# Two value products of the first key block joined into one over two segments, and issued behind both score steps of their slot

## The chip, the cores and the metric

The kernel runs on one core of a Trainium2 chip. The metric is the device time of one execution in microseconds, as the median of several runs. The engines named below are PE (TensorE, with its weight loads listed apart as PEld), DVE (VectorE), ACT (ScalarE), POOL (GpSimd), and SP, whose queue issues most of the DMAs.

## The reference

Two encoder layers over 512 tokens of width 1024, in float32. Each layer has an attention part with two groups of heads that read the same normed input, and a dense part.

```
s  = einsum('bhmqd,bhmkd->bhmqk', q, k) * scale          # differential group: 4 heads, 2 maps each
p  = softmax(where(chunk(k) <= chunk(q), s, min))
out = (p[:, :, 0] - lam * p[:, :, 1]) @ v                # v is 128 wide
z  = einsum('bhqd,bhkd->bhqk', q, k) * scale             # stick-breaking group: 8 heads
w  = where(k < q, sigmoid(z) * exp(sum of log_sigmoid(-z) over the keys between), 0)
out = w @ v                                              # v is 64 wide
```

Both groups are causal (the differential group by chunks of 64 keys), so a block of 128 queries needs only the key blocks up to its own. The outputs of both groups are joined, multiplied by `w_o` and added to x; then follow a norm, a product with 1024x4096 weights, a squared ReLU, and a product back to 1024.

## The kernel before, in words

Products are made of two or three matmuls on fp32r halves: a value is split into a high part (ACT rounds it) and a low part (DVE subtracts), and `three` (L297 to L301) issues high by high, high by low, low by high.

**Dense work and attention share PE.** In each layer the projections (`p..d1q`, `p..s0k`, `p..u` and so on) and the output projection `wo` are a generator of steps of three matmuls or so. The attention is a second generator, `attn` (L732). A loop pays out credit for each dense step and takes attention steps as long as there is credit, so on PE an attention piece is usually followed by 3 to 9 dense matmuls. The Tile layer then sets the final order on each engine by its own estimate of when things are ready; on PE it keeps nearly the written order, on DVE and ACT it moves more.

**Attention by slots.** A layer has 24 units: the 4 differential heads (kind d) with two halves of the queries each, then the 8 stick-breaking heads (kind s) with two halves each. The half 0 is queries 0 to 255, the half 1 queries 256 to 511. Slot i does three things:

- scores of unit i (`s1_df`, `s1_sb`): two or four products into PSUM tiles S, each followed by DVE and ACT work (for d: a maximum on DVE, an exp on ACT, then a combination on DVE; for s: two sigmoids on ACT, a scan on DVE, a product on POOL). Each score step is one step of the generator.
- turning of unit i-2 (`s2`): transposes on PE into the PSUM tiles T, which ACT and DVE split into SBUF tiles of turned weights. xh and xl (896 wide) hold key block 0 of half 0 at columns 0 to 255, key block 1 at 256 to 639, and key block 0 of half 1 at 640 to 895; zh and zl hold key blocks 2 and 3. There is one buffer of each.
- values of unit i-3 (`s3`): products of v with the turned weights into a PSUM tile O (one bank). Half 0 does key block 0 for queries 0 to 255. Half 1, one slot later, does key block 0 for queries 256 to 511 and key block 1 first, then blocks 2 and 3, and evicts O.

So slots with an odd i do the values of a half 0, and slots with an even i, from slot 4, those of a half 1. In such an even slot the generator `attn` interleaves: first score step, values of blocks 0 and 1, second score step, turning, values of blocks 2 and 3.

**PSUM.** The tiles S have three banks in rotation. The transposes of the head norms (rs_d, rb_d) take banks from the same three. A tile takes the bank of the third tile before it, and its first product waits until that tile's last reader is done: the exp or the second sigmoid on ACT for S, the reduction `ms<-rs_d` on DVE for rs_d, and the copy `rb` on ACT for rb_d.

**Weights.** Each dense unit's weights come by DMA (raw), ACT rounds them (whi, L116) and DVE subtracts (wlo, L132). whi and wlo have two buffers, so whi of a unit waits for the last product that reads whi two units before.

Of the kernel before, what the change touches and what calls it, by code (L numbers as in the profile page):

```python
# [9 lines left out]
F32 = mybir.dt.float32  # L10
F32R = mybir.dt.float32r
BF16 = mybir.dt.bfloat16
AF = mybir.ActivationFunctionType
# [4 lines left out]
P = 128  # L18
S = 512
# [12 lines left out]
LAG2, LAG3, KSB = 2, 3, 8  # L32
MTB = 1
# [131 lines left out]
def trunk(ctx, tc, opened, xT, w, w2, w1, gfin, lamv, cos, sin, out):  # L165
    nc = tc.nc
# [23 lines left out]
    x = cp.tile([P, KC, S], F32, tag="x", name="x")  # L190
# [38 lines left out]
    gsub = cp.tile([P, L], F32, tag="gsub", name="gsub")  # L229
# [7 lines left out]
    def split(hi, lo, src):  # L237
        a = nc.scalar.activation(hi, src, AF.Copy)  # L238
        nc.vector.tensor_tensor(out=lo, in0=src, in1=hi.bitcast(F32), op=ALU.subtract)  # L239
        return a  # L240
# [94 lines left out]
    for l in range(L):  # L335
        with ExitStack() as actx:
            am = actx.enter_context(tc.tile_pool(name=f"am{l}", bufs=1))
            ap_ = actx.enter_context(tc.tile_pool(name=f"at{l}", bufs=1))
            a2 = actx.enter_context(tc.tile_pool(name=f"a2{l}", bufs=2))
            a3 = actx.enter_context(tc.tile_pool(name=f"a3{l}", bufs=2))  # L340
# [122 lines left out]
            heads = {}  # L463
# [174 lines left out]
                yield (0.77 if half else 0.33) + (also() if also else 0.0)  # L638

            def s3(u, parts_):  # L640
                half, b, m, kind = u["half"], u["b"], u["m"], u["kind"]
                key = (kind, b, m)
                if half == 0:
                    heads[key] = bank("o", f"O{l}{kind}{b}{m}")
                k = 2 if kind == "s" else 3
                cost = 0.0
                for kb in parts_:
                    t, at_, to, w = {
                        (0, 0): ((xh, xl), 0, 0, 256), (1, 0): ((xh, xl), 640, 256, 256), (1, 1): ((xh, xl), 256, 128, 384),
                        (1, 2): ((zh, zl), 256, 256, 256), (1, 3): ((zh, zl), 0, 256, 256)}[(half, kb)]  # L650
                    o = heads[key][:, to : to + w]
                    wh, wl = (e[:, at_ : at_ + w] for e in t)
                    if kind == "s":
                        v = vs[:, kb, 2 * b + m, :]
                        nc.tensor.matmul(o, v, wh, start=(half == 0), stop=False)
                        nc.tensor.matmul(o, v, wl, start=False, stop=(kb == 3))
                    else:
                        three(o, (vd_hi[:, kb, b * P : (b + 1) * P], vd_lo[:, kb, b * P : (b + 1) * P]), (wh, wl),
                              half == 0, kb == 3)
                    cost += w * k * MMC  # L660
                if half == 1 and parts_[-1] != 3:
                    yield cost
                    return
                if half == 1:
                    o = heads.pop(key)
                    if kind == "s":
                        if m == 0:
                            heads[("mt", b)] = a2.tile([P, S], F32, tag="mt", name=f"mt{l}{b}", bufs=MTB)
                        mt = heads[("mt", b)]
                        oc = tt(f"oc{l}{b}{m}")[0:64, :]  # L670
                        nc.scalar.copy(oc, o[64:128, :])
                        nc.vector.tensor_add(mt[64 * m : 64 * m + 64, :], o[0:64, :], oc)
                        if m == 1:
                            split(ms_hi[:, b, :], ms_lo[:, b, :], mt)
                    else:
                        os_ = a2.tile([P, S], F32, tag="mt", name=f"os{l}{b}", bufs=MTB)
                        sqo = tt(f"sqo{l}{b}")
                        nc.scalar.activation(sqo, o, AF.Square)
                        nc.scalar.activation(os_, o, AF.Copy, scale=gsub[:, l : l + 1])
                        rc = a3.tile([P, 4], F32, tag="rc", name=f"rc{l}{b}")  # L680
                        late.append((b, os_, sqo, rc))
                yield cost

            units = []
# [13 lines left out]
            late = []  # L698
# [29 lines left out]

            def values(u, parts_):
                while not ok(("v" + u["kind"], u["b"])):  # L730
                    yield 0
                yield from s3(u, parts_)  # L732

            def attn():
                n = len(units)
                stage = 0
                for i in range(n + LAG3):
                    stage = stage + 1 if late else 0
                    rest = behind_scores(i, stage)
# [110 lines left out]
        with ExitStack() as fctx:  # L850
# [343 lines left out]
            for g in range(GROUPS):  # L1194
# [184 lines left out]
```

## Time and profile before

| | us |
|---|---|
| median of 3 runs | 1125.02 |
| lowest and highest run | 1124.52, 1125.22 |
| the profiled execution | 1125.43 |
| its span, first to last instruction | 1123.7 |
| PE busy in it | 1115.3 |
| DVE busy | 905.5 |
| ACT busy | 683.8 |
| POOL busy | 155.7 |

The first layer's attention fills 43 to 215 us of the span, that of the second layer 597 to 771 us. Times in rows of the timeline are from the start of the span. A matmul's row shows its start and a modelled duration; what a matmul costs a busy PE is the distance from its start to the next one's. "[0.72 <-PE p0u L438]" behind a row is the idle time of the engine before it and what ended it. Buffer numbers are left out of the names in the profile, while the lists of order below keep them (S0d_1057 is one tile).

### The profile page before, as it was taken

To read this page: it belongs to the slowest core of one execution; us is meant where nothing else is said; L and a number is where in the kernel's file an instruction comes from. 1 tells how busy PE (TensorE), PEld (TensorE's weight loads), DVE (VectorE), ACT (ScalarE), POOL (GpSimd) and SP (SyncE) were. 2 spreads that over 40 slices of the span, in tenths; PEclk is the share of its full clock that TensorE was granted. 3 is DMA by queue.
4 is the path that set the end of the run, shared out by engine and by line. 5 is a ranking of instruction groups with operands and counts; after the bars stand their busy time and mean duration, and the time that the engine had idled before them with its cause. 6 is when DMAs were issued, how large, how long until landed. Compare 5 with 4: busy or idle time off the path is not lost.

```text
span 1123.7 us, 17281 instructions
## 1 busy us (share of the span) xinstructions
PE 1115.3 (99%) x6421; PEld 979.2 (87%) x6421; DVE 905.5 (81%) x1309; ACT 683.8 (61%) x1107; POOL 155.7 (14%) x233
## 2 busy tenths in 40 slices
PE   9999999999999999999999999999999999999997
PEld 7889889888899899899878898988887998998986
DVE  7788789798668779778877887898877787797787
ACT  6446666667558457467344666665765584674665
POOL 1001344101001001001000014430010110010010
PEclk9999999999999999999999999999999999999999
DMA  7466343268687678748325654522477886687462
GB/s 256 129 190 185 113 135 111 75 226 224 175 213 183 175 192 187 190 131 218 101 75 155 191 146 132 165 61 72 150 193 212 213 188 174 186 185 205 115 131 94
DMA packets 61044, 181.26 MB, mean 161 GB/s; under 512 B 7456, under 2 KB 8736, under 8 KB 60960
## 3 DMA queue, kind: packets, MB, share of 16 engines
q1 hardware_dynamic: 50160, 141.84, 39.6%
q0 software_dynamic: 10368, 37.75, 18.9%
q8 instruction: 51, 0.84, 0.3%
q10 hardware_dynamic: 432, 0.56, 0.1%
q14 instruction: 33, 0.27, 0.1%
HBM read 150.77 MB, written 4.19 MB: 138 GB/s over the span
## 4 chain that ended last, share of the span: by engine, by line
PE 92%; DVE 3%; DMA 2%; issue 1%; ACT 1%; POOL 0%; POOLq 0%; DVEq 0%; ACTq 0%
PE X L299 9%; PE X L301 9%; PE X L300 9%; PE V L299 3%; PE V L301 3%; PE V L300 3%; PE wo L299 3%; PE wo L300 3%; PE wo L301 3%; PE Y L301 2%; PE Y L299 2%; PE Y L300 2%; DMA q<-in_w 2%; DVE wlo L132 1%; PE f L299 1%; PE f L300 1%
## 5 line engine op out<-in xcount | busy, mean ns | idle before, releaser
L116 ACT ACTIVATE whi<-q 128x1024 fp32r<-128x1024 f32 x96 | 101.5, 1059 | 110.9 <-PE X L301 38.3
L132 DVE TENSOR_TENSOR wlo<-q,whi 128x1024 fp32r<-128x1024 f32 x96 | 117.0, 1222 | 50.6 <-ACT whi L116 50.5
L132 DVE TENSOR_TENSOR wlo<-raw,whi 128x1024 fp32r<-128x1024 f32 (+1 forms) x82 | 99.1, 1215 | 9.5 <-ACT whi L116 9.0
L116 ACT ACTIVATE whi<-raw 128x1024 fp32r<-128x1024 f32 (+1 forms) x82 | 80.7, 993 | 33.4 <-issue 9.9
L299 PE MATMUL X<-whi,Ah 128*128 128x512 f32 x248 | 97.7, 394 | 0.2 <-DVE y L1107 0.2
L300 PE MATMUL X<-wlo,Ah 128*128 128x512 f32 x248 | 96.7, 390 | 0.0
L301 PE MATMUL X<-whi,Al 128*128 128x512 f32 x248 | 96.7, 390 | 0.0
L132 DVE TENSOR_TENSOR wlo<-waves,whi 128x1024 fp32r<-128x1024 f32 x40 | 48.9, 1222 | 16.5 <-ACT whi L116 16.4
L116 ACT ACTIVATE whi<-waves 128x1024 fp32r<-128x1024 f32 x40 | 42.2, 1055 | 29.1 <-PE X L301 18.2
L299 PEld LDWEIGHTS X<-whi,Ah 128*128 128x128 f32 x248 | 46.6, 188 | 12.1 <-DVE y L1107 2.0
L301 PEld LDWEIGHTS X<-whi,Al 128*128 128x128 f32 x248 | 46.6, 188 | 9.9
L300 PEld LDWEIGHTS X<-wlo,Ah 128*128 128x128 f32 x248 | 46.6, 188 | 8.9
L301 PE MATMUL X<-h_hi,wlo 128*128 128x256 f32 x192 | 54.3, 283 | 0.0
L299 PE MATMUL X<-hxh,whi 128*128 128x256 f32 x192 | 54.3, 283 | 0.0
L300 PE MATMUL X<-hxl,whi 128*128 128x256 f32 x192 | 54.3, 283 | 0.0
L301 PE MATMUL X<-hxh,wlo 128*128 128x256 f32 x192 | 54.3, 283 | 0.0
L300 PE MATMUL X<-h_lo,whi 128*128 128x256 f32 x192 | 54.3, 283 | 0.0
L299 PE MATMUL X<-h_hi,whi 128*128 128x256 f32 x192 | 54.3, 283 | 0.0
L299 PE MATMUL f<-h_hi,whi 128*128 128x512 f32 x128 | 50.3, 393 | 0.0
L301 PE MATMUL f<-h_hi,wlo 128*128 128x512 f32 x128 | 49.9, 390 | 0.0
L300 PE MATMUL f<-h_lo,whi 128*128 128x512 f32 x128 | 49.8, 389 | 0.0
L239 DVE TENSOR_TENSOR Al<-x,Ah 128x512 fp32r<-128x512 f32 (+1 forms) x60 | 46.6, 793 | 3.8 <-ACT Ah L238 3.5
(748 smaller groups left out, 3726.4 us busy)
## 6 DMA issues: line engine op xcount, KB each, us to landing
raw<-in_w SPq DMA_DIRECT2D x78, 512.0 KB, 3.6
q<-in_w SPq DMA_DIRECT2D x48, 512.0 KB, 4.2
q<-in_w POOLq DMA_DIRECT2D x48, 512.0 KB, 7.8
waves<-in_w SPq DMA_DIRECT2D x28, 512.0 KB, 4.4
first_a<-in_w SPq DMA_DIRECT2D x12, 512.0 KB, 4.6
first_b<-in_w SPq DMA_DIRECT2D x12, 512.0 KB, 5.6
first_c<-in_w SPq DMA_DIRECT2D x12, 512.0 KB, 4.2
first_b<-in_w POOLq DMA_DIRECT2D x12, 512.0 KB, 7.0
```

The lines of the kernel that those rows point to most:

```text
L116: return self.nc.scalar.activation(o, src, AF.Copy)
L132: self.last = h, nc.vector.tensor_tensor(out=lo[:, a:b], in0=raw[:, a:b], in1=hi[:, a:b].bitcast(F32), op=ALU.subtract)
L239: nc.vector.tensor_tensor(out=lo, in0=src, in1=hi.bitcast(F32), op=ALU.subtract)
L299: nc.tensor.matmul(pt, ah, bh, start=first, stop=False, skip_group_check=goes_on),
L300: nc.tensor.matmul(pt, ah, bl, start=False, stop=False, skip_group_check=goes_on),
L301: nc.tensor.matmul(pt, al, bh, start=False, stop=last, skip_group_check=goes_on))
```

## The change

Three things are changed, all in the attention part.

1. The four tiles xh, xl, zh and zl become parts of one tile `turned_` (2816 wide). That makes it possible to address the two places of key block 0 (columns 0 to 255 and 640 to 895) as one operand of two segments, `firsts`.
2. The values of half 0 are gone as a step of their own. Half 1 multiplies key block 0 for all 512 queries in one product over the two segments. For a d head three matmuls of 256 columns and three more of 256 become three of 512; for an s head two and two become two.
3. In the even slots that do values (`lead`), the generator issues the first score step, the second score step, then the values of blocks 0 and 1, the turning, and the values of blocks 2 and 3. In odd slots no values are left.

```diff
-            xh, xl = (ap_.tile([P, 896], F32R, tag=f"x{n}", name=f"x{n}{l}") for n in "hl")
-            zh, zl = (ap_.tile([P, 512], F32R, tag=f"z{n}", name=f"z{n}{l}") for n in "hl")
+            turned_ = ap_.tile([P, 2816], F32R, tag="turned", name=f"turned{l}")
+            xh, xl, zh, zl = (turned_[:, a:b] for a, b in ((0, 896), (896, 1792), (1792, 2304), (2304, 2816)))
+            firsts = [turned_[:, a : a + 1280].rearrange("p (a t) -> p a t", a=2)[:, :, 0:256] for a in (0, 896)]
...
             def s3(u, parts_):
-                half, b, m, kind = u["half"], u["b"], u["m"], u["kind"]
+                b, m, kind = u["b"], u["m"], u["kind"]
                 key = (kind, b, m)
-                if half == 0:
+                if parts_[0] == 0:
                     heads[key] = bank("o", f"O{l}{kind}{b}{m}")
                 k = 2 if kind == "s" else 3
                 cost = 0.0
                 for kb in parts_:
-                    t, at_, to, w = {
-                        (0, 0): ((xh, xl), 0, 0, 256), (1, 0): ((xh, xl), 640, 256, 256), (1, 1): ((xh, xl), 256, 128, 384),
-                        (1, 2): ((zh, zl), 256, 256, 256), (1, 3): ((zh, zl), 0, 256, 256)}[(half, kb)]
-                    o = heads[key][:, to : to + w]
-                    wh, wl = (e[:, at_ : at_ + w] for e in t)
+                    if kb == 0:
+                        o, w, (wh, wl) = heads[key], S, firsts
+                    else:
+                        t, at_, to, w = {
+                            1: ((xh, xl), 256, 128, 384), 2: ((zh, zl), 256, 256, 256), 3: ((zh, zl), 0, 256, 256)}[kb]
+                        o = heads[key][:, to : to + w]
+                        wh, wl = (e[:, at_ : at_ + w] for e in t)
...
             def behind_scores(i, stage):
                 n = len(units)
                 u = units[i - LAG3] if 0 <= i - LAG3 < n else None
-                if u and u["half"] == 1:
+                u = u if u and u["half"] else None
+                if u:
                     yield from values(u, (0, 1))
...
                 if u:
-                    yield from values(u, (2, 3) if u["half"] else (0,))
+                    yield from values(u, (2, 3))
...
                         front = (s1_sb if u["kind"] == "s" else s1_df)(u)
+                        lead = i >= LAG3 and units[i - LAG3]["half"]
                         for cost in front:
                             if i == 7 and len(u["w"]) == 2:
                                 table(AF.Sigmoid, ends["exp"])
                             yield cost
+                            if lead:
+                                lead = 0
+                                continue
                             nxt = 0
```

PE in slot 6 of the first layer (the fourth differential head begins; the values are those of the second head). Before, the products of the tile S0d_1082 are followed by dense products p0u and the values O0d_1046; the second score step, S0d_1145, comes only after 22 dense and 6 value products:

```order
L544 MATMUL S0d_1082<-st0d3k,st0d3q 128x128
L436 MATMUL p0u_1106<-whi_992,h_hi 128x256
L437 MATMUL p0u_1106<-wlo_993,h_hi 128x256
L545 MATMUL S0d_1082<-kl0d3k,st0d3q 128x128
L438 MATMUL p0u_1106<-whi_992,h_lo 128x256
L436 MATMUL p0u_1106<-whi_992,h_hi 128x256
L437 MATMUL p0u_1106<-wlo_993,h_hi 128x256
L438 MATMUL p0u_1106<-whi_992,h_lo 128x256
L299 MATMUL O0d_1046<-xh_142,vdh_140 128x256
```

Now, with the numbers of the tiles shifted (S0d_1072 is the first step's tile, S0d_1111 the second's):

```order
L545 MATMUL S0d_1072<-st0d3k,st0d3q 128x128
L438 MATMUL p0u_1096<-wlo_979,h_hi 128x256
L439 MATMUL p0u_1096<-whi_978,h_lo 128x256
L437 MATMUL p0u_1096<-whi_978,h_hi 128x256
L438 MATMUL p0u_1096<-wlo_979,h_hi 128x256
L439 MATMUL p0u_1096<-whi_978,h_lo 128x256
L546 MATMUL S0d_1072<-kl0d3k,st0d3q 128x128
L437 MATMUL p0u_1096<-whi_978,h_hi 128x256
L545 MATMUL S0d_1111<-st0d3k,st0d3q 128x256
```

The second score step now follows one dense product behind the first. The values (three of 512 columns, then three of 384) come 11 dense products later.

ACT at the same place. Before, the exp of S0d_1057, the third tile before S0d_1145, stands ahead of the rounding of a weight unit:

```order
L601 ACTIVATE p0d_1036,sm0d_978<-S0d_1033,sm0d_978 128x384
L601 ACTIVATE p0d_1060,top_867<-S0d_1057,sm0d_1056 128x512
L116 ACTIVATE whi_1108<-raw_892 128x1024
L601 ACTIVATE p0d_1070,sm0d_1056<-S0d_1067,sm0d_1056 128x512
L238 ACTIVATE hl0s0q<-t0s0k 128x512
```

Now (S0d_1044 is that third tile before, whose bank S0d_1111 takes):

```order
L602 ACTIVATE p0d_1033,sm0d_987<-S0d_1030,sm0d_987 128x384
L116 ACTIVATE whi_1098<-raw_869 128x1024
L602 ACTIVATE p0d_1047,top_874<-S0d_1044,sm0d_1043 128x512
L238 ACTIVATE hl0s0q<-t0s0k 128x512
L602 ACTIVATE p0d_1060,sm0d_1043<-S0d_1057,sm0d_1043 128x512
```

The rounding of the weights has moved ahead of the exp whose end frees the bank. The raw weights of that unit replace those of the unit p0s0k, which is two units back.

DVE in slot 11 (the norm of the fourth differential head is begun; the reduction of rs_d_1632 frees a bank of the same three). Before:

```order
L562 TENSOR_SCALAR C0s_1608<-keep0s_1606,edge 128x384
L487 TENSOR_SCALAR t0s2q<-p0s2q,norms 128x512
L132 TENSOR_TENSOR wlo_1647<-raw_1432,whi_1646 128x1024
L239 TENSOR_TENSOR xl_143<-T0s_1617,xh_142 128x512
L239 TENSOR_TENSOR zl_145<-T0s_1618,zh_144 128x384
L273 TENSOR_REDUCE ms<-rs_d_1632 128x4
```

Now:

```order
L488 TENSOR_SCALAR t0s2q<-p0s2q,norms 128x512
L132 TENSOR_TENSOR wlo_1609<-raw_1420,whi_1608 128x1024
L563 TENSOR_SCALAR C0s_1596<-keep0s_1594,edge 128x384
L239 TENSOR_TENSOR hl0s2q<-t0s2q,hl0s2q 128x512
L239 TENSOR_TENSOR turned_142<-T0s_1617,turned_142 128x512
L239 TENSOR_TENSOR turned_142<-T0s_1618,turned_142 128x384
L273 TENSOR_REDUCE ms<-rs_d_1632 128x4
```

One more subtraction of 128x512 (hl0s2q) has moved ahead of the reduction, and on ACT the rounding of that unit's weights stands ahead of the two sigmoids of S0s_1603 where it stood behind them before. The tile that takes the bank of rs_d_1632 is that of slot 12's second score step.

More of the change, by code (lines that the diff above doesn't have):

```diff
@@ L647, in s3 @@
                 for kb in parts_:
-                    t, at_, to, w = {
-                        (0, 0): ((xh, xl), 0, 0, 256), (1, 0): ((xh, xl), 640, 256, 256), (1, 1): ((xh, xl), 256, 128, 384),
-                        (1, 2): ((zh, zl), 256, 256, 256), (1, 3): ((zh, zl), 0, 256, 256)}[(half, kb)]
-                    o = heads[key][:, to : to + w]
-                    wh, wl = (e[:, at_ : at_ + w] for e in t)
+                    if kb == 0:
[5 more added lines that the diff above has]
+                        wh, wl = (e[:, at_ : at_ + w] for e in t)
                     if kind == "s":
                         v = vs[:, kb, 2 * b + m, :]
-                        nc.tensor.matmul(o, v, wh, start=(half == 0), stop=False)
+                        nc.tensor.matmul(o, v, wh, start=kb == 0, stop=False)
                         nc.tensor.matmul(o, v, wl, start=False, stop=(kb == 3))
@@ L658, in s3 @@
                         three(o, (vd_hi[:, kb, b * P : (b + 1) * P], vd_lo[:, kb, b * P : (b + 1) * P]), (wh, wl),
-                              half == 0, kb == 3)
+                              kb == 0, kb == 3)
                     cost += w * k * MMC
-                if half == 1 and parts_[-1] != 3:
+                if parts_[-1] != 3:
                     yield cost
                     return
[L664 to L681, printed above, removed]
@@ new lines, in s3 @@
+                o = heads.pop(key)
+                if kind == "s":
+                    if m == 0:
+                        heads[("mt", b)] = a2.tile([P, S], F32, tag="mt", name=f"mt{l}{b}", bufs=MTB)
+                    mt = heads[("mt", b)]
+                    oc = tt(f"oc{l}{b}{m}")[0:64, :]
+                    nc.scalar.copy(oc, o[64:128, :])
+                    nc.vector.tensor_add(mt[64 * m : 64 * m + 64, :], o[0:64, :], oc)
+                    if m == 1:
+                        split(ms_hi[:, b, :], ms_lo[:, b, :], mt)
+                else:
+                    os_ = a2.tile([P, S], F32, tag="mt", name=f"os{l}{b}", bufs=MTB)
+                    sqo = tt(f"sqo{l}{b}")
+                    nc.scalar.activation(sqo, o, AF.Square)
+                    nc.scalar.activation(os_, o, AF.Copy, scale=gsub[:, l : l + 1])
+                    rc = a3.tile([P, 4], F32, tag="rc", name=f"rc{l}{b}")
+                    late.append((b, os_, sqo, rc))
```

## Prediction

> **What bounds the kernel now.** I read the page first, for the engine without slack.
>
> ```profile
> span 1123.7 us, 17281 instructions
> ...
> PE 1115.3 (99%) x6421; PEld 979.2 (87%) x6421; DVE 905.5 (81%) x1309; ACT 683.8 (61%) x1107; POOL 155.7 (14%) x233
> ...
> PEclk9999999999999999999999999999999999999999
> ...
> PE 92%; DVE 3%; DMA 2%; issue 1%; ACT 1%; POOL 0%; POOLq 0%; DVEq 0%; ACTq 0%
> ```
>
> PE is busy 99% of the span at full clock, and 92% of the chain that ended last is PE. A change pays or costs only by what it takes off PE's own work and by the waits it brings to PE. Busy time of the stretches of the first attention shows what stands closest behind PE.
>
> ```profile
> core 0: us, PE busy (x) PEld busy (x) DVE busy (x) ACT busy (x) POOL busy (x), PEclk, DMA share, GB/s
> 70.00:104.00 34.00, 34.00 (x209) 30.44 (x208) 31.38 (x83) 20.70 (x57) 1.79 (x2) 1.00 0.73 206
> 104.00:146.00 42.00, 42.00 (x257) 37.47 (x256) 32.02 (x56) 28.50 (x59) 13.97 (x20) 1.00 0.35 107
> ```
>
> PE has no gap there, so no value product and no score step waits today. DVE is busy 31.38 of 34 us from 70 to 104 us. There the differential heads' scores need their maximum on DVE and their exp on ACT before a bank is free, and a score step that comes earlier finds a DVE with 8% to spare.
>
> **Step 1, fewer and wider products.** The price of a matmul on a busy PE is the distance of starts. The timeline of PE where a half 0 and then a half 1 of values stood:
>
> ```profile
> 114.88 0.28 PE L299 MATMUL O0d<-xh,vdh 128*128 128x256 f32 x1
> 115.00 0.28 PE L300 MATMUL O0d<-xl,vdh 128*128 128x256 f32 x1
> ...
> 115.23 0.34 PE L299 MATMUL O0d<-xh,vdh 128*128 128x384 f32 x1
> 115.41 0.34 PE L300 MATMUL O0d<-xl,vdh 128*128 128x384 f32 x1
> ...
> 115.76 0.39 PE L299 MATMUL p0s1q<-h_hi,whi 128*128 128x512 f32 x1
> 115.99 0.40 PE L300 MATMUL p0s1q<-h_lo,whi 128*128 128x512 f32 x1
> ```
>
> 256 columns take 0.12 us, 384 take 0.18, 512 take 0.23. Joined are 4 d heads with 3 pairs and 8 s heads with 2 pairs, 28 pairs a layer and 56 in all. A pair goes from 2 x 0.12 = 0.24 to 0.23 us. At 0.24 - 0.227 (the median distance I get behind a 512-wide `three` is 227 ns; the row above, rounded, gives 0.23) a pair saves 13 ns, **56 x 0.013 = 0.73 us**. No row has an operand of two segments. Its bounds are 0.227 us (a plain 512) and 0.24 us (the two it replaces), so the saving lies between 0 and 0.73 us; I take 0.73, since two runs of 256 neighbouring columns resemble the plain 512. All of it lies on the path, because PE has no gap.
>
> The Trainium skill's page "TensorE: Matmul & The Clock Gate", section "Back-to-back issue gap", gives a sustained spacing of about 131 ns for N=512 and 81 ns for N=128 in streams of weight load and matmul. Taken halfway for 256 columns that is an estimate of 65 ns saved a pair, 3.6 us in all. The rows here, 0.23 us for 512, do not agree, and I go by them.
>
> **Step 2, values moved from odd slots into even ones.** The turned weights of half 0 are read one slot later. They are overwritten only after a turning that stands behind these values on PE, so no new wait. O is claimed two score steps later than before, behind the same eviction, so that cover grows. The wider product needs the same tiles that key block 0 of half 1 needed. No DMA is issued by the step. Cost 0.
>
> **Step 3, the second score step ahead of the values.** Each S tile takes the bank of the third before it. Summing row distances in the two orders from a tile's last product to the first product that takes its bank, the room shrinks in slot 6 from 5.8 to 2.7 us and in slot 8 from 4.9 to 2.7; for the bank of rs_d in slots 10 and 12 it falls from 7.3 and 6.2 to 4.0. Four places a layer are tight, and I walk each one.
>
> *Slot 6.* Before, PE, ACT and the claim:
>
> ```profile
> 94.90 0.39 PE L300 MATMUL p0s0k<-h_lo,whi 128*128 128x512 f32 x1
> 95.13 0.39 PE L301 MATMUL p0s0k<-h_hi,wlo 128*128 128x512 f32 x1
> 95.36 0.22 PE L544 MATMUL S0d<-st0d3k,st0d3q 128*128 128x128 f32 x1
> ...
> 99.54 0.28 PE L544 MATMUL S0d<-st0d3k,st0d3q 128*128 128x256 f32 x1
> ```
> ```profile
> 94.72 0.69 ACT L601 ACTIVATE p0d<-S0d,sm0d 128x512 f32<-128x512 f32 x1 [0.41 <-DVE sm0d L607]
> ...
> 95.40 1.05 ACT L116 ACTIVATE whi<-raw 128x1024 fp32r<-128x1024 f32 x1
> 96.35 0.67 ACT L601 ACTIVATE p0d<-S0d,sm0d 128x512 f32<-128x512 f32 x1
> ```
>
> The exp that frees the bank ended at 95.41, and the claim came at 99.54: 4.1 us to spare. Now whi stands ahead of that exp, and whi cannot start before the last product that reads the buffer's old contents (L300 of p0s0k) is through. In slot 4 such a whi started 0.48 us after such a product:
>
> ```profile
> 77.82 0.39 PE L300 MATMUL p0d3k<-h_lo,whi 128*128 128x512 f32 x1
> ```
> ```profile
> 78.30 1.06 ACT L116 ACTIVATE whi<-raw 128x1024 fp32r<-128x1024 f32 x1 [0.37 <-ACT p0d L601]
> 79.26 0.67 ACT L601 ACTIVATE p0d<-S0d,sm0d 128x512 f32<-128x512 f32 x1
> ```
>
> So from L300 on: 0.48 to whi, 0.96 to the next start, 0.67 of exp = 2.11 us. PE's new order from L300 to the claim is L300 and L301 (0.46), a p0u (0.12), three S (0.28), five p0u (0.59), S (0.06), p0u (0.12) = 1.63 us. PE waits **0.5 us**. At the least 0, if whi's buffer frees sooner; at most 1.0, if DVE's maximum for that tile is late.
>
> The Trainium skill says of ACT and DVE that their queues are strict first in, first out ("TensorE: Matmul & The Clock Gate", section "Architectural detail: the array is 16× 32×32, not 1× 128×128"). The trace agrees: the exp at 96.35 starts as whi lets go. That rule speaks against this change, as no exp can pass a whi set ahead of it.
>
> *Slot 8.* Here ACT keeps its order, and PE loses six value products ahead of the claim.
>
> ```profile
> 112.69 0.28 PE L438 MATMUL p0u<-whi,h_lo 128*128 128x256 f32 x1
> ...
> 114.88 0.28 PE L299 MATMUL O0d<-xh,vdh 128*128 128x256 f32 x1
> ```
> ```profile
> 113.01 0.48 ACT L418 ACTIVATE vs<-p0u,rcol 128x256 fp32r<-128x256 f32 x1 [0.72 <-PE p0u L438]
> 113.39 1.05 ACT L116 ACTIVATE whi<-raw 128x1024 fp32r<-128x1024 f32 x1
> 114.33 0.68 ACT L601 ACTIVATE p0d<-S0d,sm0d 128x512 f32<-128x512 f32 x1
> ```
>
> From the last p0u at 112.69 ACT needs till 114.33 + 0.68 = 115.01, 2.32 us. The claim now stands where O0d stood, 114.88 - 112.69 = 2.19 us. Wait 0.13 and a release, **0.2 us** (0 to 0.6, if the maximum is late).
>
> *Slot 4.* The same chain as in slot 6, 2.11 us, against L300, L301 and 3 dense 512 (1.14), two S (0.17), 3 dense (0.69), S (0.06) = 2.06 us. **0.1 us** (0 to 0.5).
>
> *Slot 12.* The reduction of rs_d frees the bank.
>
> ```profile
> 139.34 0.48 PE L299 MATMUL p0s2k<-h_hi,whi 128*128 128x512 f32 x1
> ...
> 142.88 0.40 PE L299 MATMUL p0s2k<-h_hi,whi 128*128 128x512 f32 x1
> ```
> ```profile
> 140.84 1.59 DVE L132 TENSOR_TENSOR wlo<-raw,whi 128x1024 fp32r<-128x1024 f32 x1
> ...
> 143.42 0.68 DVE L273 TENSOR_REDUCE ms<-rs_d 128x4 f32<-128x512 f32 x1
> 144.02 0.68 DVE L239 TENSOR_TENSOR hl0s2q<-t0s2q,hl0s2q 128x512 fp32r<-128x512 f32 x1
> ```
>
> The reduction ended at 144.10. Between 139.34 and the claim stand 15 dense products (3.4 to 3.6) and two S pairs (0.6): 143.5. With hl0s2q (0.6) ahead of it the reduction would end at 144.7, 1.2 us late; but whi moves ahead of two sigmoids, the dense unit whose end starts this chain ends three products (0.7) sooner, and wlo at 1.59 us ran beside POOL, while its usual time is 1.22. That gives back 0.7 to 1.2. I take **0.4 us** (0 to 1.1). In slot 10 the order on DVE is unchanged and the dense unit ends sooner by 0.7 too; 0 (to 0.4).
>
> *Sum.* 0.5 + 0.2 + 0.1 + 0.4 = 1.2 us a layer; the second layer has the same order there, so 2.4 us. With -0.73 the change costs **+1.7 us**. The profiled execution took 1125.43 us (span 1123.7 and 1.7 around it) and would take 1127.1; it stands 0.4 above the median of 1125.02, so for a median I say **1126.7 us**. Upper ends together: (1.0 + 0.6 + 0.5 + 1.1 + 0.4) x 2 = 7.2 us; with no saving 1132.2. Lower ends: 1124.3.
>
> **Rivals.** *All is covered*: the waits of step 3 vanish, because the releases are quicker than my chains or DVE runs ahead; only the 0.73 us is left, 1124.3. For it speaks that each wait is small beside the 2 us chains it is a difference of; against it, that two of the four are set by PE's own products on ACT and need no backlog. *DVE's backlog decides*: from 70 to 104 us it has 2.6 us of slack in 34, and the second score steps now ask for their maxima up to 3.3 us earlier than before (sums of row distances in the order). If the waits reach 1.5 us a layer, which a delay of the maxima by some 0.3 us at each of the places does, it is slower by over 0.2%; at 2.3 us a layer it is 4.6 - 0.73 = 3.9 us, 1128.9. *The joined product is much cheaper*: were it as quick as the 384-wide row (0.18 us), a pair would save 65 ns and 56 pairs 3.6 us, 1121.4. The 512-wide row speaks against it; it is also what the skill's spacing would give. That the change did not arrive is excluded by the order.
>
> **Chances.** Small waits as forecast (1124.9 to 1127.2) 0.38; all covered 0.22; backlog 0.37; much cheaper 0.03. 0.2% is 2.25 us, about what a measurement of this kernel can tell from no change. Faster by more, below 1122.8: 0.03. Within: 0.60. Slower, above 1127.3: 0.37. The range leaves out the cheaper product and most of the sum of all upper ends: 1124.2 to 1129.2.
>
> **What would show it.** Value rows of 128x512 at a distance of 0.23, and 56 matmuls fewer (6365). Gaps on PE just before the second score step of slots 4, 6, 8 and 12, released by ACT p0d (L602) or DVE ms, about 0.5, 0.2, 0.1 and 0.4 us, the same in both layers; none before values, none before weights. Gaps of a microsecond at slots 4 to 8 with DVE full would show the backlog. I am wrong if PE waits for wlo or for T tiles, or if the two segments make the 512-wide product slower than 0.24.

## The result and the profile after

The changed kernel takes 1128.45 us (median of 7 runs, 1127.96 to 1129.09) against 1124.75 us of the kernel before (median of 7 runs; the 1125.02 us above is that of 3): +3.7 us, a ratio of 1.0032 with a 95% interval of 1.0021 to 1.0044. Two executions of the kernel lead14p below, its profiled one among them, were far longer (2865 and 1372 us), so its times are those of its other ten, and its gaps were read in a second run of the same kernel, lead14p_again. The profiled execution of the changed kernel took 1128.35 us. Its page:

```profile
span 1126.6 us, 17172 instructions
...
PE 1116.3 (99%) x6365; PEld 976.8 (87%) x6365; DVE 901.2 (80%) x1309; ACT 684.0 (61%) x1107; POOL 149.3 (13%) x233
```

There are 56 matmuls fewer, and PE still shows 99%. Shares do not show what happened; distances of starts on PE do. Beyond the usual distance, PE loses 0.2 us or more at four places in a layer, and at the same four in the other. (Start, modelled duration, engine, line, tiles; in brackets the idle time by modelled ends, which is shorter than the gap by distances.)

PE in slots 6 and 8, just ahead of the second score steps:

```profile
96.41 0.33 PE L437 MATMUL p0u<-whi,h_hi 128*128 128x256 f32 x1
97.06 0.39 PE L545 MATMUL S0d<-st0d3k,st0d3q 128*128 128x256 f32 x1 [0.31 <-ACT p0d L602]
...
115.17 0.39 PE L301 MATMUL p0s1q<-h_hi,wlo 128*128 128x512 f32 x1
115.67 0.39 PE L545 MATMUL S0s<-st0s0k,st0s0q 128*128 128x256 f32 x1
```

A 256-wide product is usually followed after 0.12 us and a 512-wide one after 0.23: the gaps are 0.65 - 0.12 = **0.53 us** and 0.50 - 0.23 = **0.27 us**. ACT at these places:

```profile
95.28 1.06 ACT L116 ACTIVATE whi<-raw 128x1024 fp32r<-128x1024 f32 x1
96.25 0.67 ACT L602 ACTIVATE p0d<-S0d,sm0d 128x512 f32<-128x512 f32 x1
...
113.90 1.05 ACT L116 ACTIVATE whi<-raw 128x1024 fp32r<-128x1024 f32 x1
114.85 0.68 ACT L602 ACTIVATE p0d<-S0d,sm0d 128x512 f32<-128x512 f32 x1
```

Both exps start as the rounding of the weights ends, and PE starts 0.14 us behind each exp's end (96.92 and 115.53).

The largest gap is in slot 24, inside the joined product, in both layers:

```profile
206.91 0.39 PE L658 MATMUL O0s<-turned,vs 128*128 128x512 f32 x1
208.14 0.50 PE L659 MATMUL O0s<-turned,vs 128*128 128x512 f32 x1 [0.83 <-DVE turned L239]
...
764.50 0.39 PE L658 MATMUL O1s<-turned,vs 128*128 128x512 f32 x1
765.72 0.50 PE L659 MATMUL O1s<-turned,vs 128*128 128x512 f32 x1 [0.83 <-DVE turned L239]
```

1.23 - 0.23 = **1.0 us**. The second matmul reads the low part of the turned weights, and DVE had not subtracted it yet. DVE and POOL there, and DVE some microseconds before:

```profile
200.96 0.88 DVE L563 TENSOR_TENSOR_SCAN C0s<-keep0s,edge 128x256 f32<-128x256 f32 x1 [0.98 <-POOL sig0s L566]
...
202.34 1.39 DVE L132 TENSOR_TENSOR wlo<-raw,whi 128x1024 fp32r<-128x1024 f32 x1
...
206.39 1.08 DVE L239 TENSOR_TENSOR vdl<-mt,vdh 128x512 fp32r<-128x512 f32 x1
207.40 1.14 DVE L239 TENSOR_TENSOR turned<-T0s,turned 128x512 fp32r<-128x512 f32 x2
```
```profile
206.07 0.86 POOL L566 TENSOR_TENSOR sig0s<-sig0s,C0s 128x384 f32<-128x384 f32 x1 [3.27 <-ACT sig0s L561]
```

The fourth gap is in slot 21, among the seven transposes T0s of a half 1, which wait for the split that reads the PSUM tile they are to overwrite. (The expectations below put it into slot 22; the score steps around it show that it is one slot earlier.)

```profile
194.86 1.18 PE L633 MATMUL T0s<-edge,sig0s 128*128 128x128 f32 x7
195.79 0.48 PE L299 MATMUL wo<-mdh,whi 128*128 128x512 f32 x1
...
204.31 0.93 PE L633 MATMUL T0s<-edge,sig0s 128*128 128x128 f32 x7
204.99 0.47 PE L299 MATMUL wo<-mdh,whi 128*128 128x512 f32 x1
```
```profile
192.19 0.89 DVE L563 TENSOR_TENSOR_SCAN C0s<-keep0s,edge 128x256 f32<-128x256 f32 x1 [0.99 <-POOL sig0s L566]
...
193.57 1.39 DVE L132 TENSOR_TENSOR wlo<-raw,whi 128x1024 fp32r<-128x1024 f32 x1
194.89 0.55 DVE L239 TENSOR_TENSOR turned<-T0s,turned 128x384 fp32r<-128x384 f32 x1
```

The seven transposes take 0.93 us in slot 21 and 0.68 in slot 23: **0.25 us**, of which one distance alone holds 0.19.

The joined product itself costs about what a plain one costs:

```profile
116.70 0.39 PE L299 MATMUL O0d<-turned,vdh 128*128 128x512 f32 x1
116.93 0.40 PE L300 MATMUL O0d<-turned,vdh 128*128 128x512 f32 x1
```

0.23 us from start to start (median 231 ns; plain dense products 227). The distances behind all value products add up to 36.44 us before and 35.99 now (six distances over 0.28 us, which hold a wait or the like, counted as 0.231): 0.45 us saved. The account is 2 x (0.53 + 0.27 + 1.0 + 0.25) - 0.45 = +3.65 us, against +3.7 measured.

The traces confirm the total without any choice of gaps. From the first score product to the first product of the dense part, the first layer takes 195.29 us before and 197.13 now, the second 196.75 and 198.63: +3.72 us in all. (The spans of the two profiled executions differ by 2.9 us only: in the dense part of the second layer PE lost 0.92 us in that of the kernel before, behind its products at 855.27 and 864.38, and nothing there in the other.) That the account by gaps closes so well is in part chance, as it leaves out two things that nearly cancel. Behind a matmul that waited in slots 6, 8 and 24 the next distance is 0.10 to 0.11 us longer than usual as well (97.06 to 97.28, 115.67 to 115.89, 208.14 to 208.47), and in slot 4 PE loses about 0.13 us. Against that, the other distances behind dense products add up to 0.34 us less in the first layer and 0.41 in the second; what makes them shorter is not shown.

### The profile page after: what moved, and what is told of

It reads as the page before. It is cut to its first block, busy times and chain, and to the rows that moved or that the text cites. A ratio compares the mean times of both kernels' runs of the same rounds, so it can differ in the third digit from the quotient of the medians.

```text
span 1126.6 us, 17172 instructions
## 1 busy us (share of the span) xinstructions
PE 1116.3 (99%) x6365; PEld 976.8 (87%) x6365; DVE 901.2 (80%) x1309; ACT 684.0 (61%) x1107; POOL 149.3 (13%) x233
## 4 chain that ended last, share of the span: by engine, by line
PE 96%; DVE 2%; ACT 1%; issue 1%; POOL 0%; POOLq 0%; DVEq 0%
PE X L299 9%; PE X L300 9%; PE X L301 9%; PE V L299 4%; PE V L300 4%; PE V L301 4%; PE f L301 3%; PE f L299 3%; PE f L300 3%; PE wo L299 2%; PE wo L301 2%; PE wo L300 2%; PE Y L301 2%; PE Y L300 2%; PE Y L299 2%; PE W L301 1%
## 5 line engine op out<-in xcount | busy, mean ns | idle before, releaser
L132 DVE TENSOR_TENSOR wlo<-raw,whi 128x1024 fp32r<-128x1024 f32 (+1 forms) x82 | 95.9, 1175 | 7.9 <-ACT whi L116 7.9
```

The lines of the kernel that those rows point to most:

```text
L132: self.last = h, nc.vector.tensor_tensor(out=lo[:, a:b], in0=raw[:, a:b], in1=hi[:, a:b].bitcast(F32), op=ALU.subtract)
```

## The experiments

In all of them times go against the kernel before on the same chip. Gaps are distances of starts on PE less the usual ones, in us, one layer (the other layer's agree within 0.01 us, except that of slot 25 in the last row, 0.10 there); a blank is less than 0.12. The ratio with its interval is the one on record; the quotient of the two medians differs from it by up to 0.0003.

| kernel | median | before beside it | ratio, 95% interval | slot 6 | 8 | 14 | 21 | 24 | 25 |
|---|---|---|---|---|---|---|---|---|---|
| changed | 1128.45 | 1124.75 | 1.0032 (1.0021 to 1.0044) | 0.53 | 0.27 | | 0.19 | 1.00 | |
| join | 1126.15 | 1125.18 | 1.0007 (0.9998 to 1.0016) | | | 0.47 | | 0.47 | |
| lead | 1126.14 | 1125.18 | 1.0009 (1.0000 to 1.0018) | | 0.27 | | | | |
| expfirst | 1126.96 | 1125.18 | 1.0015 (1.0007 to 1.0024) | | | | 0.19 | 0.99 | |
| apart | 1127.66 | 1125.18 | 1.0021 (1.0011 to 1.0030) | 0.53 | 0.27 | | 0.19 | 0.17 | 0.37 |
| splitfirst | 1126.70 | 1125.14 | 1.0012 (1.0003 to 1.0020) | 0.52 | 0.27 | | 0.19 | | |
| nolead22 | 1127.42 | 1125.14 | 1.0018 (1.0010 to 1.0027) | 0.52 | 0.27 | | 0.19 | 0.46 | |
| swaps | 1124.81 | 1125.14 | 0.9996 (0.9988 to 1.0005) | | | | 0.19 | | |
| lead14p | 1123.95 | 1125.14 | 0.9987 (0.9979 to 0.9996) | not read | not read | not read | not read | not read | not read |
| cbuf | 1127.13 | 1125.27 | 1.0014 (1.0005 to 1.0023) | 0.51 | 0.27 | | | 0.46 | |
| nolead20 | 1127.20 | 1125.27 | 1.0017 (1.0008 to 1.0026) | 0.52 | 0.27 | | | 0.54 | |
| lead14p_again | 1124.41 | 1125.27 | 0.9991 (0.9982 to 1.0000) | | | | | | 0.14 |

The intervals are some 1 us wide to either side, so the time alone does not tell gaps of 0.3 us apart. The gaps do, and where one is removed the time follows within that width.

### join: the joined product alone

```diff
-                        lead = i >= LAG3 and units[i - LAG3]["half"]
+                        lead = 0
```

> The changed kernel with the joined product alone: the second score step stands behind the values again, as before. Theory (the four gaps): the gaps ahead of the second score steps of slots 6 and 8 (0.53 and 0.27 us) are gone in both layers, the gap of 1.0 us inside the values of slot 24 stays, because no score step stands there to lead, and a new one of 0.3 to 0.7 us may come in slot 14, where the split of the turned weights had ended only 0.5 us ahead of the 384-wide product before: 2 x (1.0 + 0.5 + 0.2) - 0.73 = +2.7 us against before (2.0 to 3.3). Rival (all of the loss comes from the second score step being early): no gap is left, -0.7 us. Rival (the loss is a price of the two-segment operand): +3.7 us, with value rows of 512 columns spaced wider than 0.24 us.

Measured: +1.0 us, less than the 2.0 to 3.3 expected. PE, the joined product in slots 14 and 24:

```profile
155.05 0.39 PE L658 MATMUL O0s<-turned,vs 128*128 128x512 f32 x1
155.74 0.50 PE L659 MATMUL O0s<-turned,vs 128*128 128x512 f32 x1 [0.30 <-DVE turned L239]
...
205.83 0.39 PE L658 MATMUL O0s<-turned,vs 128*128 128x512 f32 x1
206.53 0.50 PE L659 MATMUL O0s<-turned,vs 128*128 128x512 f32 x1 [0.31 <-DVE turned L239]
```

The gaps of slots 6 and 8 are gone, the one in slot 14 came as expected, and that of slot 24 is there without any early score step, but at 0.47 us and not at 1.0. So the joined product has waits of its own, and the early score step doubles one of them. The rival by which the score step is all of it falls, and so does the one by the price of the operand.

### lead: the early score step alone

To the kernel before:

```diff
+                        lead = i >= LAG3 and units[i - LAG3]["half"]
                         for cost in front:
...
                             yield cost
+                            if lead:
+                                lead = 0
+                                continue
```

> The kernel before with the early second score step alone: the values of half 0 stay a step and a product of their own in the odd slots. Theory: gaps of 0.5 us in slot 6 and 0.3 us in slot 8, none in slot 24, in both layers: +1.6 us against before (1.2 to 2.2). Rival (all of the loss comes from the second score step being early): +3.7 to +4.4 us. Rival (the joined product is what costs): 0.

Measured: +1.0 us, a little less than the 1.2 to 2.2 expected. The gap of slot 8 is there, none in slot 24, and, against what I expected, none in slot 6. On ACT the exp still stands ahead of the rounding here, and ends at 95.53:

```profile
94.84 0.69 ACT L601 ACTIVATE p0d<-S0d,sm0d 128x512 f32<-128x512 f32 x1 [0.38 <-DVE sm0d L607]
...
95.52 1.05 ACT L116 ACTIVATE whi<-raw 128x1024 fp32r<-128x1024 f32 x1
```

The gap of slot 6 needs both parts: the joined product shifts the work so that the order on ACT turns over, and the early score step then waits for it. The gaps of the two parts alone (0.94 and 0.27 us a layer) do not add up to the 2.0 of both, and in slot 21 the joined product alone has no gap and the early score step alone one of 0.10 us.

### expfirst: two roundings put behind the exp on ACT

```diff
         h = self.round(hi[:, a:b], raw[:, a:b])
+        if b == 1024 and (_UNITS[i][0],) + _UNITS[i][2:] in (("v", 1024, 1), ("p", 640)):
+            self.behind(h, _CTX["exps"][-2])
...
                                 ends["exp"] = nc.scalar.activation(
                                     pp[:, 0:wd], ss[:, 0:wd], AF.Exp, bias=sm[:, mm : mm + 1],
                                     accum_out=sums[mm])
+                                _CTX.setdefault("exps", []).append(ends["exp"])
```

> The changed kernel, with the rounding of two weight units a layer (the second half of the first value projection, and the key projection of the second stick-breaking head pair) put behind the exp of the fourth differential heads' bank on ACT. PE's order is the same. Theory (the exp waits in ACT's queue behind the rounding): the gaps of 0.53 us in slot 6 and 0.27 us in slot 8 are gone, the 1.0 us of slot 24 and the 0.19 of slot 22 stay: -1.6 us against the changed kernel, +2.1 us against before. Rival (the maximum on DVE, not ACT's queue, sets the exp): the gaps stay, +3.7. Rival (the weights then come late): a gap of about 0.5 us ahead of the first product of those units.

Measured: +1.8 us against before. PE's order differs by one dense product. ACT and PE in slot 6:

```profile
95.91 0.69 ACT L604 ACTIVATE p0d<-S0d,sm0d 128x512 f32<-128x512 f32 x1
```
```profile
97.02 0.22 PE L548 MATMUL S0d<-kl0d3k,st0d3q 128*128 128x128 f32 x1
97.08 0.34 PE L547 MATMUL S0d<-st0d3k,st0d3q 128*128 128x256 f32 x1
```

The exp ends at 96.60, ahead of the claim at 97.08, and both gaps are gone while the other two stay. No product waits for the later weights. The theory of ACT's queue holds, and neither rival does.

### apart: one head's values as before

```diff
-                u = u if u and u["half"] else None
-                if u:
+                u = u if u and (u["half"] or i == 23) else None
+                if u and u["half"]:
                     yield from values(u, (0, 1))
...
-                    yield from values(u, (2, 3))
+                    yield from values(u, (2, 3) if u["half"] else (0,))
...
-                    if kb == 0:
+                    if kb == 0 and own:
+                        at_, w = (640 if u["half"] else 0), 256
+                        o = heads[key][:, 256 * u["half"] : 256 * u["half"] + 256]
+                        wh, wl = (e[:, at_ : at_ + w] for e in (xh, xl))
+                    elif kb == 0:
```

(`own` is the seventh stick-breaking head.)

> The changed kernel, with the values of the seventh stick-breaking head alone done as before: its half 0 as a step of its own in slot 23, its half 1 in slot 24. Theory (in slot 24 the values of half 0 and the dense products behind them were the cover for the split of the turned weights on DVE): two products and three dense ones, 0.92 us, stand again between the turning and the first product of slot 24, and the gap of 1.0 us shrinks to 0.1 (0 to 0.3) in both layers: -1.8 us against the changed kernel, +1.9 us against before. Rival (DVE's backlog, not the order on PE, sets it, and moves along): the gap stays above 0.5 us or opens again in slot 26.

Measured: +2.5 us. The gap of slot 24 shrinks from 1.0 to 0.17, as the cover returns, but a new one of 0.37 us opens in slot 25, among the transposes:

```profile
212.39 0.47 PE L299 MATMUL wo<-mdh,whi 128*128 128x512 f32 x1
212.98 0.55 PE L633 MATMUL T0s<-edge,sig0s 128*128 128x128 f32 x3
```

The theory and its rival each held in part: the two products and the dense ones behind them were the cover, and DVE's lateness is not cured by cover; the next thing on PE that needs DVE finds it late (the transposes of slot 25 go on at 212.98, 0.06 us after a split on DVE that reads a tile T has ended).

### splitfirst: one swap on DVE

```diff
                         split(ms_hi[:, b, :], ms_lo[:, b, :], mt)
+                        heads["low"] = W.low
...
                     split(xh[:, 384:896], xl[:, 384:896], pts[0])
+                    if (u["kind"], u["b"], u["m"]) == ("s", 3, 0):
+                        behind(heads["low"], W.low)
```

(`W.low` is the subtraction that `split` issued last.)

> The changed kernel with one swap on DVE in each layer: the subtraction of the finished third pair of stick-breaking heads (vdl) stands behind, not ahead of, the split of the turned weights that slot 24 reads. PE and ACT keep their order. Theory (that subtraction, slowed by POOL, is what makes the split late): the split starts 1.0 us earlier, and the gap of 1.0 us in slot 24 falls to 0.2 (0 to 0.4), the gaps of slots 6, 8 and 22 stay: -1.6 us against the changed kernel, +2.1 us against before. Rival (the split would wait for ACT's half of it or for the transposes): the gap stays above 0.6 us. Rival (the wait comes back in slot 26): little change in time, +3.5.

Measured: +1.6 us against before. PE, DVE and POOL in slot 24:

```profile
206.71 0.39 PE L660 MATMUL O0s<-turned,vs 128*128 128x512 f32 x1
207.02 0.50 PE L661 MATMUL O0s<-turned,vs 128*128 128x512 f32 x1
```
```profile
206.28 0.69 DVE L239 TENSOR_TENSOR turned<-T0s,turned 128x512 fp32r<-128x512 f32 x1
206.88 0.68 DVE L239 TENSOR_TENSOR vdl<-mt,vdh 128x512 fp32r<-128x512 f32 x1
```
```profile
205.87 0.87 POOL L566 TENSOR_TENSOR sig0s<-sig0s,C0s 128x384 f32<-128x384 f32 x1 [3.27 <-ACT sig0s L561]
```

The orders of PE and ACT are those of the changed kernel. The gap is 0.31 - 0.23 = 0.08 us, and nothing opens in slot 25 or 26. What stood directly ahead of the split on DVE was the last link.

### nolead22, nolead20, cbuf: why DVE is late there

Two kernels take the early score step out of one slot each:

```diff
-                        lead = i >= LAG3 and units[i - LAG3]["half"]
+                        lead = i >= LAG3 and units[i - LAG3]["half"] and i != 22
```

> The changed kernel with the second score step of slot 22 alone put back behind the values. Theory (the early score step of slot 22 brings its sigmoids, its scan and its product on POOL forward, and so pushes DVE's later work back): the gap of 0.19 us ahead of the turning in slot 22 is gone, and that of slot 24 falls from 1.0 to the 0.47 us that the joined product has by itself; those of slots 6 and 8 stay: -1.4 us against the changed kernel, +2.3 against before. Rival (the early score steps of all slots add up to a backlog on DVE, and that of slot 22 is only the last): the gap of slot 24 stays at 0.8 to 1.0 us.

Measured: +2.3 us. The gap of slot 24 falls to 0.46 as expected. The 0.19 us stay: they lie in slot 21, ahead of the score step that was put back, and my theory had them a slot too late. The second one (`i != 20`):

> The changed kernel with the second score step of slot 20 alone put back behind the values. Theory (each gap stems from the early score step ahead of it: DVE's scan that waits for POOL in slot 20 makes the turning of slot 22 late): the gap of 0.19 us in slot 22 is gone, that of slot 24 stays at 1.0 us, as its own scan waits still: -0.4 us against the changed kernel. Rival (a backlog over several slots): the gap of slot 24 shrinks as well.

Measured: +1.9 us. The 0.19 us of slot 21 are gone, so they stem from slot 20. But that of slot 24 shrinks too, from 1.0 to 0.54, as the rival had it: lateness is handed on over four slots. DVE in slot 20's place here has no wait ahead of the scan, and the weights' subtraction goes first:

```profile
191.74 1.48 DVE L132 TENSOR_TENSOR wlo<-raw,whi 128x1024 fp32r<-128x1024 f32 x1
193.14 0.90 DVE L563 TENSOR_TENSOR_SCAN C0s<-keep0s,edge 128x256 f32<-128x256 f32 x1
```

In the changed kernel the early step's scan stood ahead of that subtraction and waited 0.99 us for POOL, with all that is queued behind it. The scan writes a tile C, of which there are two, and must wait until POOL's product has read the one it takes. The third kernel gives it a tile of its own and changes the order on POOL alone:

```diff
-                    C = a3.tile([P, S + 1], F32, tag="C", name="C" + nm)
+                    C = a3.tile([P, S + 1], F32, tag="C", name="C" + nm) if i != 1 else a3.tile(
+                        [P, 257], F32, tag="C1", name="C" + nm, bufs=1)
```

> The changed kernel with one more buffer: the scan of the 256-wide score rows (second score step of a half 0) has a tile C of its own, in place of taking turns with the two of the other scans. The orders of PE, ACT and DVE are unchanged. Theory (the early second score step puts its scan ahead of the weights' subtraction on DVE; the scan waits about 1.0 us for POOL's product to free C, and all that stands behind it on DVE is late): DVE's idle time ahead of the 256-wide scan in slots 20 and 22 is gone, the gap of 0.19 us in slot 22 is gone, and that of 1.0 us in slot 24 falls to 0.5 or less; those of slots 6 and 8 stay: -1.4 us against the changed kernel (-1.0 to -2.4), +2.3 against before. Rival (the scan would wait for its sigmoid anyway): the idle time and the gaps stay.

Measured: +1.9 us. DVE and PE:

```profile
198.87 2.10 DVE L564 TENSOR_TENSOR_SCAN C0s<-keep0s,edge 128x512 f32<-128x512 f32 x3
...
201.48 1.47 DVE L132 TENSOR_TENSOR wlo<-raw,whi 128x1024 fp32r<-128x1024 f32 x1
```
```profile
207.31 0.39 PE L659 MATMUL O0s<-turned,vs 128*128 128x512 f32 x1
207.99 0.50 PE L660 MATMUL O0s<-turned,vs 128*128 128x512 f32 x1 [0.30 <-DVE turned L239]
```

Three scans run without a break, the gap of slot 21 is gone, and that of slot 24 is 0.46, what the joined product has without any early score step. So the chain is shown: early score step, a scan that waits for a buffer of C ahead of the weights on DVE, a late split, a waiting PE. It makes 0.54 of the 1.0 us in slot 24 and all of the gap in slot 21. The other 0.46 belong to the joined product and the subtraction vdl ahead of the split.

### swaps and lead14p: both swaps, and a version without the gaps

`swaps` is the changed kernel with the edits of expfirst and splitfirst together.

> The changed kernel, with the two roundings a layer put behind the exps on ACT as in the run above and the swap on DVE as in the run before; the early second score step stays in all slots. Theory: only the gaps of slot 22 (0.19) and what is left in slot 24 (0.2) remain in each layer: 2 x 0.4 - 0.7 = 0.1 us against before (-0.5 to +0.6), -3.6 us against the changed kernel. Rival (the waits depend on one another): one of the removed gaps comes back, +1 us or more.

Measured: -0.3 us against before (0.9996, 0.9988 to 1.0005), which is no change clear of the noise. Only the gap of slot 21 is above 0.12 us. The four tiles of turned weights are one tile here too, so making them one brings no wait that shows. PE does the same value products and the same early score steps as in the changed kernel, in the same order but for one dense product a layer; four moved instructions on ACT and two on DVE in the whole program, with what the scheduler shifted around them, take away the loss.

`lead14p` keeps the early step only where the joined product needs it, and puts dense work ahead of slot 24:

```diff
-                        lead = i >= LAG3 and units[i - LAG3]["half"]
+                        lead = i == 14
...
+                if i == 24:
+                    yield 0.6
                 if u:
                     yield from values(u, (0, 1))
```

> The joined product everywhere, the early second score step in slot 14 alone (where the joined product by itself has a gap of 0.47 us), and three dense products put ahead of the values of slot 24. Theory: no gap in slots 6, 8, 14 and 22; in slot 24 the 0.69 us of dense products cover the 0.47 us; only the cheaper product is left: -0.7 us against before (-0.9 to 0). Rival (a gap removed on PE opens at the next place that waits for DVE): gaps of 0.3 us or more in slots 14 to 26, 0 to +1.5 us.

Measured: -1.2 us (0.9987, 0.9979 to 0.9996), a little below the -0.9 to 0 expected. The same kernel once more:

> The kernel of the run before with the early score step in slot 14 alone and the dense products ahead of slot 24, for a profile that nothing disturbed. Theory: no gap above 0.12 us in the attention of either layer, and -0.3 to -1.5 us against before.

Measured: -0.9 us (0.9991, 0.9982 to 1.0000). The largest gap in the attention is 0.14 us, in slot 25 of one layer, so the waits are gone. This version is at or just below the kernel before. By its trace the two attention parts, from the first score product to the first product of the dense part, are 0.67 us shorter than before. The distances behind value products make 0.15 us of that (36.29 us in place of 36.44); where the rest comes from is not shown.

## Why the prediction came out as it did

I gave 1126.7 us and a range of 1124.2 to 1129.2. The time lies in the range, on the slower side as forecast, 1.75 us above the likeliest value. By change against before it was +1.7 forecast and +3.7 measured, 0.32% slower: the outcome to which I gave 0.37, not the one that I held likeliest. That the time lies in the range is in part luck. The terms for slots 4, 6 and 8 were about right, those for the saving and for slot 12 too high, and two waits, in slots 24 and 21, were missing; the 0.4 us a layer put too high for slot 12 hide part of the 1.25 us a layer that were missing.

- **Step 1**, the products. The mechanism is right: 512 columns over two segments cost 231 ns. The term was mis-sized: -0.45 us for the -0.73. Two 256-wide products cost 237 ns and not 240, and the wide one 231 and not 227, so the 56 pairs save 6 ns each, 0.34 us; small shifts behind other value products make the rest of the 0.45. The estimate of 65 ns a pair from the two spacings cited in that step has a slip as well: halfway between them gives 81 ns a pair and 4.5 us. Nothing in the sum rests on it.
- **Step 2, "Cost 0", is the step that failed.** I looked at who overwrites the turned weights and at the claim of O, and not at what stands between the split and its first reader. In slot 24 of the kernel before there were two value products and three dense ones of half 0, 0.93 us, between the turning and that reader:

```profile
205.65 0.68 DVE L239 TENSOR_TENSOR xl<-T0s,xh 128x512 fp32r<-128x512 f32 x1
```
```profile
206.38 0.28 PE L655 MATMUL O0s<-xh,vs 128*128 128x256 f32 x1
...
207.31 0.28 PE L655 MATMUL O0s<-xh,vs 128*128 128x256 f32 x1
207.43 0.28 PE L656 MATMUL O0s<-xl,vs 128*128 128x256 f32 x1
```

  The split ended at 206.33, the reader came at 207.43: 1.1 us to spare, of which the step takes 0.93. In the other slots the second score step takes the place of that cover. Slot 24 has no scores left. join shows the price by itself (0.47 us there and in slot 14), apart shows the cover coming back. The step is answerable for 0.46 of the 1.0 us.
- **Step 3 failed too, in what it left out.** I followed the early score step to the banks of S alone, and not its scan into DVE's queue. There it waits about 1.0 us for a tile C, and what stands behind it is late: that makes the other 0.54 us in slot 24 and the gap of slot 21 (cbuf).
- **Step 3, slot 6**: 0.5 forecast, 0.53 measured, and by the mechanism named (expfirst). lead adds that the order on ACT which causes it came with the joined product. My chain had no release in it, which is 0.14 us; the chain came out 0.04 us shorter than I had it, and PE's products ahead of the claim 0.05 longer. **Slot 4**: 0.1 forecast, about 0.13 measured: the exp ended at 79.81 and the claim came at 79.95, the same 0.14 us behind it as in slots 6 and 8. That is 0.03 later than usual, and the next distance is 0.10 longer (0.22 and not 0.12); by this count slots 6 and 8 lose 0.63 and 0.37. **Slot 8**: 0.2 and 0.27, right. **Slot 10**: none, right. **Slot 12**: 0.4 and none. The reduction ended at 145.17, later than any of my values, but the claim came at 145.44:

```profile
144.49 0.68 DVE L273 TENSOR_REDUCE ms<-rs_d 128x4 f32<-128x512 f32 x1
```
```profile
139.41 0.40 PE L299 MATMUL p0s2k<-h_hi,whi 128*128 128x512 f32 x1
...
145.44 0.28 PE L545 MATMUL S0s<-st0s1k,st0s1q 128*128 128x256 f32 x1
```

  From the start of p0s2k to the claim are 6.0 us; I had 4.2. The transposes T0s and rs_d and three more dense products now stand behind that start, and I had moved the dense unit forward without them.
- **The rivals.** "All is covered" was wrong. "DVE's backlog decides" gave 1128.9, near the 1128.45 that came, but from another place: the maxima of slots 4 to 8 never were late enough, while the scans of slots 20 and 22 were, by waiting for POOL. I had called new waits for T tiles a sign of being wrong, and slot 21 has one; I had also named no wait at the values, and slot 24 has the largest of all there.

## What to carry to other kernels

A product that is taken out is also cover for the work behind which it stood; go through every place where it stood, the last turn of a pipeline first, as there may be nothing left to take its place. Where work is issued earlier, follow it to every queue that it enters: here a scan that came early on DVE and waited for a buffer held up everything behind it, and PE met that four slots later. When the gaps are known, they can be removed by reordering the engine that holds the late link, with PE's own order left almost alone.

## What the runs showed of the hardware

A subtraction on DVE with both inputs in SBUF (vdl<-mt,vdh, 128x512) takes 0.67 to 0.69 us by itself. Where it was issued while a product ran on POOL it took 1.06 to 1.09 (in the changed kernel at 206.39, POOL's product running from 206.07 to 206.93: it held on for the 0.54 us that POOL still needed and ran 0.54 more). Where POOL's product came second it was POOL's that grew, from 0.86 to between 1.13 and 1.17 us, and the subtraction took 0.67. In the kernel before, the subtraction of slot 24 was the first of the two:

```profile
205.07 0.67 DVE L239 TENSOR_TENSOR vdl<-mt,vdh 128x512 fp32r<-128x512 f32 x1
205.32 1.13 POOL L565 TENSOR_TENSOR sig0s<-sig0s,C0s 128x384 f32<-128x384 f32 x1 [2.56 <-ACT xh L238]
```

In the changed kernel it was the second (1.08 us), and that is 0.4 us of the late split. The split with one input in PSUM (turned<-T0s, 128x512) took 0.66 to 0.69 us in all 24 cases of the changed kernel, 14 of them beside a POOL product, as the row at 206.28 in splitfirst. The Trainium skill ("Trainium Architecture — The Big Picture", section "What this means for kernel authors") says that DVE and GpSimd share a port pair by an exclusive lock. The subtraction agrees with that: whoever came second took longer. In those 14 cases of the split, which reads one of its two inputs from PSUM, the split took no longer, and neither did POOL's product where the split came first (0.86 to 0.87 us).

Each of the changed kernel's four gaps came back in both layers within 0.01 us, and in the other kernels that kept it within 0.02 us (slot 6 0.51 to 0.53, slot 8 0.27, slot 21 0.19). So in these traces gaps of 0.2 us could be read one by one where the median cannot tell them. Outside the attention that did not hold: the 0.92 us that PE lost in the dense part of one execution are not in the other.
